# One block of an RWKV-7 layer: v's transposition moved, the last bonus moved, copies of the recurrence shared by ScalarE and VectorE

## The chip, the cores and the metric

The kernel runs on one core of a Trainium2 chip. The metric is the device time of one execution, in microseconds (us). The engines are named as in the profile: PE (TensorE, matrix products), DVE (VectorE), ACT (ScalarE), POOL (GpSimd) and SP (SyncE, which only issues DMAs here). Each engine works through its own queue in order, and a semaphore holds an instruction until what it needs is there.

## The reference, cut to what matters

One layer over 4096 tokens of width 1024, in fp32. An RMS-normalised, modulated input h is projected at once for a pooling branch and for the RWKV-7 branch (512 wide, 8 heads of 64). Around the change lies the second one:

```
seg = seg + (prev - seg) * mu_shift                  # each token mixed with the one before
r, w_lo, k, v, a_lo, z = split(seg)
decay = exp(-exp(-softplus(-(w0 + tanh(w_lo) @ w_up)) - 0.5))
a  = sigmoid(a0 + a_lo @ a_up);  kk = normalise(k * k_k);  k = k * (1 + (a - 1) * k_a)
# per head, token by token, S is 64 x 64:
sa = S @ (-kk);  S = S * decay + sa (kk * a)^T + v k^T;  y = S @ r
y  = groupnorm(y) * ln_w + ln_b
bonus = sum(r * k * r_k) * v
y_rwkv = (y + bonus) * silu(z)
out = concat(y_pool, y_rwkv) @ w_out;  x = rmsnorm(x + gate * out) * final_g
```

## The kernel before

The program has three stages. Until about 345 us it normalises x, transposes h to DRAM as two fp16 halves (high and low) and does the pooling branch (`proj`, L411 to L418). From there to about 1750 us it does the RWKV branch in 16 blocks of 256 tokens. Then comes the output projection (`project`, L923 to L965). The change lies in the middle stage.

A block has 4 chunks of 64 tokens and its 8 heads form 4 pairs. The recurrence is done chunk by chunk: within a chunk, the 64 steps are a triangular system, whose inverse is applied with matmuls. For each block b these functions run:

- `front(b, f)`, L542 to L649: a generator that projects the 17 segments of the block (pj, tile number m). Segment 0 holds the inputs of decay and a (lo), then pair p has k, r, v and z, m = 1+4p to 4+4p. A segment (`seg`) is 24 fp16 matmuls of 128x257 into a PSUM tile, evicted by an ACT activation (L561) and a DVE multiply-add with the shifted tokens (L562). After a pair's r segment come pl and pa (L588, L589), the tanh of both on ACT (tw, ta), the scan over time on DVE (L596) and the exponentials Ppad and Pi (L598, L600); after its v segment the DVE work that fills AR and BK, the operands of the scores (L608 to L619). Two closures remain from each pair: `cent`, which transposes v with two matmuls into vps (L629) and copies it with ACT into UV (L635), in the last pair with the squared norms of k (L632) as well, and `late`, which multiplies rk with a matrix of ones (pb, L642) and that by v on DVE (bon, L643). Both go on a list `todo`, which the next pair works off, `cent` ahead of its v segment and `late` behind it; those of the last pair are worked off in `scores`.
- `scores(b, f, fill)`, L651 to L693: for each chunk eight matmuls of BK with AR (scp), masked by DVE (L671), and in chunk 2 the norms (d2).
- `inverse`, L695 to L765: Ab is transposed out of the scores by DVE (L708), 30 dependent steps of two small DVE instructions follow (L726, L731), then the results are transposed, copied by ACT (MQ, L757) and completed by matmuls (qp, m21p); btp transposes BK on PE.
- `chain`, L795 to L865: for each chunk, the state S times AR (px, L814), two copies to SBUF (xa, L821), the matmuls with the inverse (psn, L826), two copies to SBUF (UV, L834), the update of the state (L842, and L848 on DVE), the output (L853) and two copies of it (y, L860). In each of these three pairs the two copies read the two halves of the partitions, one 64 x 256 each. Behind them runs the group norm of the output (gn, L866 to L878, with rstd on POOL at L875) and its transposition (ytp, L889) and last steps (mx, L891 to L893).

The front of block b+1 runs inside the other functions of block b: each `fill(n)` lets it issue n more steps, one k of a segment at a time. A scheduler then orders the instructions of each engine; some (`tc.high_priority`) are preferred, and the matmuls of the recurrence keep the order of the program. The pool of PSUM tiles `ps_pj` has three buffers, which pj, pl, pa, vps, pb and the output projection take in turn. So a new pj waits until the tile three before it has been read.

Of the kernel before, what the change touches and what calls it, by code (L numbers as in the profile page):

```python
# [25 lines left out]
HS = 64  # L26
# [26 lines left out]
def kernel(  # L53
# [29 lines left out]
    V, A, G, PE, SP = nc.vector, nc.scalar, nc.gpsimd, nc.tensor, nc.sync  # L83
# [56 lines left out]
    with ExitStack() as ph:  # L140
# [182 lines left out]
        for tok in plan.split():  # L323
            op, q = tok[0], int(tok[1:] or 0)
# [160 lines left out]
    with ExitStack() as ph:  # L485
# [56 lines left out]
        def front(b, f):  # L542
# [33 lines left out]
            todo = []  # L576
            sqs = []
            for p in range(NPAIR):
                kS = yield from seg(1 + 4 * p, "kS")
                sq = wk.tile([P, TB2], F32, tag=f"sq{p}", name=f"sq{b}_{p}")  # L580
                sqs.append(sq)
                A.activation(sq, kS, AF.Square, scale=vec[:, V_KK + p : V_KK + p + 1])
                yield
                rS = yield from seg(2 + 4 * p, "rS")

# [12 lines left out]
                A.activation(Pp[:, :, 1:], c3(L), AF.Exp, bias=0.0, scale=cexp)  # L598
                Pi = wk.tile([P, TB2], F32, tag="Pi", name=f"Pi{b}_{p}")
                A.activation(Pi, L, AF.Exp, bias=0.0, scale=-cexp)  # L600
                if todo:
                    todo.pop(0)()
                yield
                vS = yield from seg(3 + 4 * p, "vS")
                if p == 0:
# [39 lines left out]
                todo = [cent, late]  # L645
# [5 lines left out]
        def scores(b, f, fill):  # L651
            AR, BK = f["AR"], f["BK"]

            d2 = sm.tile([64, NI], F32, tag="d2", name=f"d2_{b}")
            d2T = sm.tile([P, 32], F32, tag="d2T", name=f"d2T{b}")
            sc = blk.tile([P, NI, P], F32, tag="sc", name=f"sc{b}")
            BT = blk.tile([P, NCH, 512], F32, tag="BT", name=f"BT{b}")
            for ch in range(NCH):

                pts = [pool.tile([P, 512], F32, tag=tg, name=f"scp{b}_{ch}_{tg}") for pool, tg in ((ps_sc, "sc"), (ps_x, "px"))]  # L660
                for j in range(4):
                    for hq in range(2):
                        o = 64 * hq
                        PE.matmul(  # L664
                            pts[hq][:, j * P : (j + 1) * P],
                            BK[o : o + 64, j, ch].rearrange("q a t -> q (a t)"),
                            AR[o : o + 64, j, ch].rearrange("q a t -> q (a t)"),
                            start=True, stop=True,
                        )
                for hq in range(2):  # L670
                    V.tensor_mul(  # L671
                        sc[:, ch * NH : (ch + 1) * NH, :].rearrange("q (j h) t -> q j h t", h=2)[:, :, hq],
                        pts[hq].rearrange("q (j t) -> q j t", j=4),
                        mask.unsqueeze(1).to_broadcast([P, 4, P]),
                    )
                fill(FS + 1)
                if ch == 2:
                    pt = ps_sc.tile([P, 512], F32, tag="sc", name=f"d2p{b}")
                    for c_ in range(NCH):
                        PE.transpose(pt[:64, c_ * P : (c_ + 1) * P], ssb[:, c_ * C : (c_ + 1) * C], ident)  # L680
                    V.tensor_scalar_max(
                        d2.rearrange("q (c p h) -> q c p h", c=NCH, h=2),
                        pt[:64].rearrange("q (c p e) -> q c p e", c=NCH, e=32)[:, :, :, 0:2], L2_EPS * L2_EPS,
                    )
                    V.reciprocal(d2, d2)
                    for g in range(2):
                        V.transpose(d2T[64 * g : 64 * g + 64], d2)
                if ch in (0, 3):
                    f["todo"].pop(0)()
                fill(FS)  # L690
                if ch % 2 == 0:
                    run(gns[0], 1)
            f["sc"], f["BT"], f["d2T"] = sc, BT, d2T  # L693
# [75 lines left out]
        def ordered(mm):  # L769

            pin[0] = True
            return tc.keep_in_program_order(mm)
# [22 lines left out]
        def chain(b, f, fill):  # L795
            AR, UV, sc, BT, pc = f["AR"], f["UV"], f["sc"], f["BT"], f["pc"]
            MT = UV[0:64].rearrange("q c (h t) -> q (c h) t", h=NH)
            pe, po = f["px"]
            uo = 4 * HS
            for ch in range(NCH):  # L800
                par = 256 * (ch % 2)

                psn = ps_s.tile([P, 512], F32, tag="psn", name=f"psn{b}_{ch}")
                if ch % 2 == 0:
                    y = blk.tile([P, 512], F32, tag="y", name=f"y{b}_{ch}", bufs=3)
                yv = y[64 * (ch % 2) : 64 * (ch % 2) + 64].rearrange("q (j f e) -> q j f e", f=2, e=HS)
                uv = UV[0:64, ch, :].rearrange("q (j f e) -> q j f e", f=2, e=HS)

                for p in range(NPAIR):
                    cs = slice(par + p * HS, par + (p + 1) * HS)  # L810
                    for ar in range(2):
                        for hf, px in ((0, pe), (1, po)):
                            o, ro = 64 * hf, 64 * (hf ^ ar)
                            ordered(PE.matmul(  # L814
                                px[ro : ro + 64, cs], AR[o : o + 64, p, ch, ar, :], S[o : o + 64, p, :],
                                start=(p == 0 and ar == 1), stop=(ar == 0), skip_group_check=True,
                            ))
                xa = blk.tile([64, 2, 256], F32, tag="W", name=f"xa{b}_{ch}")
                for hf, px in ((0, pe), (1, po)):
                    with tc.high_priority(offset=PRI):  # L820
                        A.copy(xa[:, hf, :], px[64 * hf : 64 * hf + 64, par : par + 256])  # L821
                fill(FA)
                nl = lead(b, f, ch + 1) if ch + 1 < NCH else iter(())
                for p in range(NPAIR):
                    for hf in range(2):
                        ordered(PE.matmul(  # L826
                            psn[64 * hf : 64 * hf + 64, uo + p * HS : uo + (p + 1) * HS],
                            MT[:, ch * NH + 2 * p + hf, :], xa[:, hf, p * HS : (p + 1) * HS],
                            start=True, stop=True, skip_group_check=True,
                        ))  # L830
                    run(nl, 1)
                for hf in range(2):
                    with tc.high_priority(offset=PRI):
                        A.copy(uv[:, :, hf], psn[64 * hf : 64 * hf + 64, uo:].rearrange("q (j e) -> q j e", e=HS))  # L834
                run(gns[0], 1)

                Sd = blk.tile([P, NPAIR, HS], F32, tag="Wt", name=f"Sd{b}_{ch}")
                V.tensor_mul(Sd, S, pc[:, :, ch : ch + 1].to_broadcast([P, NPAIR, HS]))
                fill(FB)
                for h in range(NH):  # L840
                    o, e = 64 * (h % 2), slice(h * HS, (h + 1) * HS)
                    ordered(PE.matmul(  # L842
                        psn[o : o + 64, (h // 2) * HS : (h // 2 + 1) * HS], BT[:, ch, e], UV[:, ch, e],
                        start=True, stop=True, skip_group_check=True,
                    ))
                with tc.high_priority(offset=PRI):
                    for p in range(NPAIR):
                        V.scalar_tensor_tensor(  # L848
                            S[:, p, :], psn[:, p * HS : (p + 1) * HS], pc[:, p, ch : ch + 1], Sd[:, p, :], op0=ALU.mult, op1=ALU.add,
                        )  # L850
                for h in range(NH):
                    hf, o = h % 2, 64 * (1 - h % 2)
                    ordered(PE.matmul(  # L853
                        (pe, po)[hf][o : o + 64, par + (h // 2) * HS : par + (h // 2 + 1) * HS],
                        sc[:, ch * NH + h, 64:128], UV[:, ch, h * HS : (h + 1) * HS],
                        start=False, stop=True, skip_group_check=True,
                    ))
                for hf, px in ((0, pe), (1, po)):
                    o = 64 * (1 - hf)
                    A.copy(yv[:, :, hf], px[o : o + 64, par : par + 256].rearrange("q (j e) -> q j e", e=HS))  # L860
                run(gns[0])
                if ch % 2 == 1:
                    gns[0] = gn(b, f, ch // 2, y)
                    run(gns[0], 1)
                fill(FY)  # L865
# [49 lines left out]
        def run(g, n=100000):  # L915
            for _ in range(n):
                if next(g, run) is run:
                    return
# [48 lines left out]
        gns = [iter(())]  # L967
        fs = {0: {}}
        run(front(0, fs[0]))
        for b in range(NB2):  # L970
            f = fs[b]
# [80 lines left out]
```

## Time and profile before

| what | us |
|---|---|
| median of 3 runs | 2130.35 |
| lowest and highest run | 2128.62, 2130.52 |
| the profiled execution | 2131.77 |
| its span | 2130.1 |

TensorE's mean granted clock over the span was 0.979 of full speed. The page gives each engine's busy time over the whole span. It says nothing of which engine sets the pace in a stage; that is read from the chain of waits and from what each engine waits for in one stretch. Times in the rows below are us from the span's start, one block of the middle stage being the stretch from 983.62 to 1068.53. The granted clock (PEclk) is a share of 2.4 GHz: 1.00 is that, 0.50 is 1.2 GHz.

### The profile page before, as it was taken

To read this page: it belongs to the slowest core of one execution; us is meant where nothing else is said; L and a number is where in the kernel's file an instruction comes from. 1 tells how busy PE (TensorE), PEld (TensorE's weight loads), DVE (VectorE), ACT (ScalarE), POOL (GpSimd) and SP (SyncE) were. 2 spreads that over 40 slices of the span, in tenths; PEclk is the share of its full clock that TensorE was granted. 3 is DMA by queue.
4 is the path that set the end of the run, shared out by engine and by line. 5 is a ranking of instruction groups with operands and counts; after the bars stand their busy time and mean duration, and the time that the engine had idled before them with its cause. 6 is when DMAs were issued, how large, how long until landed. Compare 5 with 4: busy or idle time off the path is not lost.

```text
span 2130.1 us, 48341 instructions
## 1 busy us (share of the span) xinstructions
PE 1984.4 (93%) x20186; PEld 1464.5 (69%) x20186; DVE 1454.7 (68%) x3549; ACT 966.0 (45%) x2119; POOL 148.3 (7%) x270
## 2 busy tenths in 40 slices
PE   3999999998999999999989999999899989999998
PEld 1544444577777777777777777777777767788886
DVE  7898877466867768678687686685776866533333
ACT  2544533244455554554555545545555453312111
POOL 3000000000000000000000000000001000100000
PEclk7999999999999999999999999999999999999999
DMA  7876767300100100101101001011010334443421
GB/s 277 279 237 208 256 209 268 97 21 2 32 27 6 31 15 18 32 2 31 27 6 31 23 10 32 2 31 27 7 31 27 134 111 140 150 142 133 152 106 69
DMA packets 140444, 183.19 MB, mean 86 GB/s; under 512 B 12097, under 2 KB 94017, under 8 KB 140226
## 3 DMA queue, kind: packets, MB, share of 16 engines
q1 hardware_dynamic: 140226, 180.11, 25.7%
q8 instruction: 158, 2.59, 0.5%
q14 instruction: 60, 0.49, 0.1%
HBM read 121.22 MB, written 58.85 MB: 85 GB/s over the span
## 4 chain that ended last, share of the span: by engine, by line
PE 54%; DVE 28%; ACT 10%; issue 4%; DMA 2%; POOL 0%; SPq 0%; DVEq 0%; ACTq 0%; POOLq 0%
PE po L952 6%; PE po L954 5%; PE po L953 5%; PE pj L557 5%; DVE W L731 4%; PE pj L559 4%; PE pj L558 4%; DVE Wt L726 4%; PE pp L415 4%; PE pp L416 4%; PE pp L417 4%; DVE Ab L708 3%; PE psn L826 2%; PE scp_sc L664 2%; PE px L814 2%
## 5 line engine op out<-in xcount | busy, mean ns | idle before, releaser
L557 PE MATMUL pj<-hh,w2h 128*128 128x257 f16 x2176 | 609.4, 280 | 49.8 <-DVE bon L643 23.9
L559 PE MATMUL pj<-hh,w2l 128*128 128x257 f16 x2176 | 603.9, 278 | 0.0
L558 PE MATMUL pj<-hl,w2h 128*128 128x257 f16 x2176 | 601.9, 277 | 0.0
L558 PEld LDWEIGHTS <-w2h 128*128 128x128 f16 x2176 | 217.5, 100 | 89.0 <-issue 59.1
L557 PEld LDWEIGHTS <-w2h 128*128 128x128 f16 x2176 | 214.8, 99 | 52.2 <-issue 6.5
L559 PEld LDWEIGHTS <-w2l 128*128 128x128 f16 x2176 | 213.4, 98 | 34.0
L952 PE MATMUL po<-wo,mh 128*128 128x512 f32 x512 | 204.3, 399 | 3.7 <-ACT mh L936 3.7
L953 PE MATMUL po<-wo,mh 128*128 128x512 f32 x512 | 201.9, 394 | 0.0
L416 PE MATMUL pp<-lo,w1h 128*128 128x512 f16 x512 | 195.1, 381 | 1.4 <-DVE lo L228 1.4
L415 PE MATMUL pp<-hi,w1h 128*128 128x512 f16 x512 | 194.9, 382 | 0.8 <-ACT hi L227 0.8
L417 PE MATMUL pp<-hi,w1l 128*128 128x512 f16 x512 | 195.0, 381 | 0.0
L956 DVE TENSOR_TENSOR x<-po,x 128x512 f32<-128x512 f32 x64 | 44.2, 690 | 151.5 <-PE po L954 151.4
L958 ACT ACTIVATE sq<-x 128x512 f32<-128x512 f32 x64 | 40.4, 631 | 209.2 <-DVE x L956 190.9
L726 DVE TENSOR_TENSOR Wt<-W,Ab 128x30 f32<-128x30 f32 (+7 forms) x480 | 117.6, 245 | 10.2
L731 DVE TENSOR_TENSOR W<-W,Wt 128x30 f32<-128x30 f32 (+7 forms) x480 | 117.5, 245 | 9.1
L952 PEld LDWEIGHTS po<-wo,mh 128*128 128x128 f32 x512 | 96.6, 189 | 26.0 <-ACT mh L936 3.9
L953 PEld LDWEIGHTS po<-wo,mh 128*128 128x128 f32 x512 | 96.6, 189 | 22.3
L954 PE MATMUL po<-wo,ml 128*128 128x512 f32 x256 | 101.5, 398 | 0.0
L562 DVE SCALAR_TENSOR_TENSOR kS<-pj,c,kS 128x256 f32<-128x256 f32 x64 | 30.6, 478 | 101.5 <-ACT kS L561 101.5
L417 PEld LDWEIGHTS <-w1l 128*128 128x128 f16 x512 | 50.3, 98 | 62.0 <-issue 2.8
L416 PEld LDWEIGHTS <-w1h 128*128 128x128 f16 x512 | 50.3, 98 | 60.1 <-issue 1.6
L415 PEld LDWEIGHTS <-w1h 128*128 128x128 f16 x512 | 50.4, 98 | 59.1 <-issue 1.2
(244 smaller groups left out, 3836.0 us busy)
## 6 DMA issues: line engine op xcount, KB each, us to landing
x<-in_x_dram SPq DMA_DIRECT2D x64, 256.0 KB, 2.9
out_dram<-x SPq DMA_DIRECT2D x64, 256.0 KB, 2.1
xk<-in_xT_dram SPq DMA_DIRECT2D x56, 256.0 KB, 3.8
xt<-in_x_dram SPq DMA_DIRECT2D x28, 512.0 KB, 5.6
wada<-in_w_ada_dram SPq DMA_DIRECT2D x24, 512.0 KB, 6.8
w2raw<-in_w_in_dram SPq DMA_DIRECT2D x17, 512.0 KB, 5.3
hh<-hT_hi SPq DMA_DIRECT2D x32, 257.0 KB, 3.6
hl<-hT_lo SPq DMA_DIRECT2D x32, 257.0 KB, 3.0
```

What stands on the lines that cost most here:

```text
L415: PE.matmul(pp, w1_hi[m][:, k, :], hi, start=(k == 0), stop=False)
L416: PE.matmul(pp, w1_hi[m][:, k, :], lo, start=False, stop=False)
L417: PE.matmul(pp, w1_lo[m][:, k, :], hi, start=False, stop=(k == KT - 1))
L557: unpin(PE.matmul(pp, w2_hi[m][:, k, :], hh[k], start=(k == 0), stop=False))
L558: PE.matmul(pp, w2_hi[m][:, k, :], hl[k], start=False, stop=False)
L559: PE.matmul(pp, w2_lo[m][:, k, :], hh[k], start=False, stop=(k == KT - 1))
L708: V.transpose(Ab[o : o + 32], sc[o : o + 32, :, o : o + 32].rearrange("s i t -> s t i"))
L726: V.tensor_mul(tmp[:, :n, :k], W[:, r0:, k : k + 1].to_broadcast([P, n, k]), Ab[:, k : k + 1, :k].to_broadcast([P, n, k]),)
L731: V.tensor_add(W[:, r0:, :k], W[:, r0:, :k], tmp[:, :n, :k])
L952: unpin(PE.matmul(po, mh[:, k, ts_], wo[0][k][n], start=(k == 0), stop=False))
L953: PE.matmul(po, mh[:, k, ts_], wo[1][k][n], start=False, stop=False)
L954: PE.matmul(po, (ml[:, k] if b % 2 == 0 else ml[k])[:, ts_], wo[0][k][n], start=False, stop=(k == KT - 1))
```

## The change

Three edits. `cent` of the pair before is worked off behind the next pair's k segment and no longer ahead of its v segment. `late` of the last pair is worked off in chunk 1 of the scores and no longer in chunk 3. And of each pair of copies in the recurrence (xa, UV, y) the second goes to DVE.

```diff
--- before.py
+++ after.py
@@ -580,6 +580,8 @@
                 sq = wk.tile([P, TB2], F32, tag=f"sq{p}", name=f"sq{b}_{p}")
                 sqs.append(sq)
                 A.activation(sq, kS, AF.Square, scale=vec[:, V_KK + p : V_KK + p + 1])
+                if todo:
+                    todo.pop(0)()
                 yield
                 rS = yield from seg(2 + 4 * p, "rS")
 
@@ -598,8 +600,6 @@
                 A.activation(Pp[:, :, 1:], c3(L), AF.Exp, bias=0.0, scale=cexp)
                 Pi = wk.tile([P, TB2], F32, tag="Pi", name=f"Pi{b}_{p}")
                 A.activation(Pi, L, AF.Exp, bias=0.0, scale=-cexp)
-                if todo:
-                    todo.pop(0)()
                 yield
                 vS = yield from seg(3 + 4 * p, "vS")
                 if p == 0:
@@ -685,7 +685,7 @@
                     V.reciprocal(d2, d2)
                     for g in range(2):
                         V.transpose(d2T[64 * g : 64 * g + 64], d2)
-                if ch in (0, 3):
+                if ch < 2:
                     f["todo"].pop(0)()
                 fill(FS)
                 if ch % 2 == 0:
@@ -816,9 +816,9 @@
                                 start=(p == 0 and ar == 1), stop=(ar == 0), skip_group_check=True,
                             ))
                 xa = blk.tile([64, 2, 256], F32, tag="W", name=f"xa{b}_{ch}")
-                for hf, px in ((0, pe), (1, po)):
+                for hf, px, cp in ((0, pe, A.copy), (1, po, V.tensor_copy)):
                     with tc.high_priority(offset=PRI):
-                        A.copy(xa[:, hf, :], px[64 * hf : 64 * hf + 64, par : par + 256])
+                        cp(xa[:, hf, :], px[64 * hf : 64 * hf + 64, par : par + 256])
                 fill(FA)
                 nl = lead(b, f, ch + 1) if ch + 1 < NCH else iter(())
                 for p in range(NPAIR):
@@ -829,9 +829,9 @@
                             start=True, stop=True, skip_group_check=True,
                         ))
                     run(nl, 1)
-                for hf in range(2):
+                for hf, cp in ((0, A.copy), (1, V.tensor_copy)):
                     with tc.high_priority(offset=PRI):
-                        A.copy(uv[:, :, hf], psn[64 * hf : 64 * hf + 64, uo:].rearrange("q (j e) -> q j e", e=HS))
+                        cp(uv[:, :, hf], psn[64 * hf : 64 * hf + 64, uo:].rearrange("q (j e) -> q j e", e=HS))
                 run(gns[0], 1)
 
                 Sd = blk.tile([P, NPAIR, HS], F32, tag="Wt", name=f"Sd{b}_{ch}")
@@ -855,9 +855,9 @@
                         sc[:, ch * NH + h, 64:128], UV[:, ch, h * HS : (h + 1) * HS],
                         start=False, stop=True, skip_group_check=True,
                     ))
-                for hf, px in ((0, pe), (1, po)):
+                for hf, px, cp in ((0, pe, A.copy), (1, po, V.tensor_copy)):
                     o = 64 * (1 - hf)
-                    A.copy(yv[:, :, hf], px[o : o + 64, par : par + 256].rearrange("q (j e) -> q j e", e=HS))
+                    cp(yv[:, :, hf], px[o : o + 64, par : par + 256].rearrange("q (j e) -> q j e", e=HS))
                 run(gns[0])
                 if ch % 2 == 1:
                     gns[0] = gn(b, f, ch // 2, y)
```

Two lines are added behind L582 and two taken out behind L600, so that in between a line of the changed kernel has a number two higher than before.

The order of instructions on DVE, in the recurrence of block 5, chunk 2 (Sd5_2, psn5_2), beside which the front of block 6 has its last pair (L611 to L619). Before:

```order
L872 TENSOR_REDUCE var5_0_11345<-ysq5_0_11343 128x8 [waits Activation_49]
L611 SCALAR_TENSOR_TENSOR BK6_10613<-tb6_3_11455,pv_3663,Pi6_3_11314 128x4x64 [waits DVE_49]
L873 TENSOR_SCALAR var5_0_11345<-var5_0_11345 128x8 [waits DVE_49]
L612 TENSOR_TENSOR ta6_3_11308<-ta6_3_11308,kS6_13_11207 128x256 [waits Activation_49]
L877 TENSOR_TENSOR y5_0_11155<-y5_0_11155,rstd5_0_11348 128x512 [waits Pool_49]
L613 TENSOR_TENSOR AR6_10375<-rS6_14_11299,Ppad1_3673 128x4x64
L614 TENSOR_TENSOR BK6_10613<-ta6_3_11308,Pi6_3_11314 128x4x64 [waits DVE_49]
L643 TENSOR_TENSOR bon6_10376<-pb6_2_11464,vS6_11_11009 128x256 [waits PE_49]
L619 SCALAR_TENSOR_TENSOR rk6_3_11467<-rS6_14_11299,pv_3663,ta6_3_11308 128x256
L848 SCALAR_TENSOR_TENSOR S_3678<-psn5_2_11357,pc5_9168,Sd5_2_11406 128x64 [waits PE_49,Activation_49]
```

After, with the copies of xa (L821) and UV (L834), each with what it waits for:

```order
L612 TENSOR_TENSOR ta6_3_11313<-ta6_3_11313,kS6_13_11207 128x256 [waits Activation_49]
L872 TENSOR_REDUCE var5_0_11345<-ysq5_0_11343 128x8 [waits Activation_49]
L821 COPY xa5_2_11375<-px5_1_11058 64x256 [waits PE_49]
L873 TENSOR_SCALAR var5_0_11345<-var5_0_11345 128x8 [waits DVE_49]
L613 TENSOR_TENSOR AR6_10375<-rS6_14_11304,Ppad1_3673 128x4x64
L877 TENSOR_TENSOR y5_0_11155<-y5_0_11155,rstd5_0_11348 128x512 [waits Pool_49]
L614 TENSOR_TENSOR BK6_10613<-ta6_3_11313,Pi6_3_11319 128x4x64
L643 TENSOR_TENSOR bon6_10376<-pb6_2_11464,vS6_11_11009 128x256
L834 COPY UV5_9169<-psn5_2_11357 64x4x64 [waits Activation_49]
L619 SCALAR_TENSOR_TENSOR rk6_3_11467<-rS6_14_11304,pv_3663,ta6_3_11313 128x256
L848 SCALAR_TENSOR_TENSOR S_3678<-psn5_2_11357,pc5_9168,Sd5_2_11406 128x64 [waits PE_49]
```

The UV copy stands behind L877, L614 and bon6 (L643), and waits for ACT.

On PE, at the start of the inverse of block 5: the last matmul of segment 2 of block 6, the matmuls of its first pair's decay (pl6_0, pa6_0) and the transpositions btp5. Before:

```order
L559 MATMUL pj6_2_10508<-hh6_1_10371,w2l2_959 128x257
L588 MATMUL pl6_0_10547<-lo6_0_10428,up_89 128x256
L718 MATMUL btp5_0_10561<-ident_80,BK5_9403 128x128 x4
L718 MATMUL btp5_1_10574<-ident_80,BK5_9403 128x128
L589 MATMUL pa6_0_10548<-lo6_0_10428,up_89 128x256
L718 MATMUL btp5_1_10574<-ident_80,BK5_9403 128x128 x3
L557 LDWEIGHTS w2h3_962
L557 MATMUL pj6_3_10567<-hh6_0_10367,w2h3_962 128x257
```

After:

```order
L559 MATMUL pj6_2_10511<-hh6_1_10371,w2l2_959 128x257
L590 MATMUL pl6_0_10547<-lo6_0_10428,up_89 128x256
L591 MATMUL pa6_0_10548<-lo6_0_10428,up_89 128x256
L718 MATMUL btp5_0_10561<-ident_80,BK5_9403 128x128 x4
L557 LDWEIGHTS w2h3_962
L557 MATMUL pj6_3_10567<-hh6_0_10367,w2h3_962 128x257
```

pl6_0 and pa6_0 now stand together, and the matmuls of btp5_1 follow later.

On PE, around the last pair's bonus of block 5 (pb5_3), which the scores of block 5 have worked off. Before, in segment 2 of block 6, behind the last matmuls of the scores:

```order
L558 MATMUL pj6_2_10508<-hl6_0_10369,w2h2_958 128x257
L559 LDWEIGHTS w2l2_959
L559 MATMUL pj6_2_10508<-hh6_0_10367,w2l2_959 128x257
L642 MATMUL pb5_3_10515<-rk5_3_10257,bones_3640 128x256
L557 LDWEIGHTS w2h2_958
L557 MATMUL pj6_2_10508<-hh6_0_10367,w2h2_958 128x257
```

After, between segments 0 and 1 of block 6, ahead of the matmuls of the scores' last chunks:

```order
L558 MATMUL pj6_0_10380<-hl6_1_10373,w2h0_950 128x257
L559 LDWEIGHTS w2l0_951
L559 MATMUL pj6_0_10380<-hh6_1_10371,w2l0_951 128x257
L642 MATMUL pb5_3_10432<-rk5_3_10257,bones_3640 128x256
L557 LDWEIGHTS w2h1_954
L557 MATMUL pj6_1_10435<-hh6_0_10367,w2h1_954 128x257
```

pb5_3 has moved ahead by about one segment and a half.

## Rows read from the trace of the kernel before

**Rows 1.** The page's first part, busy us, share of the span, instructions, by engine.

```profile
PE 1984.4 (93%) x20186; PEld 1464.5 (69%) x20186; DVE 1454.7 (68%) x3549; ACT 966.0 (45%) x2119; POOL 148.3 (7%) x270
```

**Rows 2.** Chain of waits, whole program: start us, duration us, engine, tile, line.

```profile
560.09 1.85 DVE Ab L708
...
983.62 1.85 DVE Ab L708
...
1068.53 1.86 DVE Ab L708
...
1152.60 1.85 DVE Ab L708
...
1661.28 1.85 DVE Ab L708
```

**Rows 3.** Stretches: start:end, length, busy (count) by engine, PEclk, DMA share, GB/s.

```profile
983.50:1025.60 42.10, 37.74 (x369) 30.41 (x367) 38.80 (x112) 21.00 (x46) 2.49 (x8) 0.96 0.03 7
1003.70:1007.00 3.30, 3.30 (x18) 2.35 (x16) 3.16 (x11) 1.32 (x3) 0.19 (x1) 0.50 0.00 0
1025.60:1051.20 25.60, 23.99 (x501) 18.09 (x499) 11.68 (x33) 17.86 (x47) 1.93 (x2) 1.00 0.03 7
1051.20:1068.50 17.30, 17.30 (x197) 14.17 (x196) 11.07 (x26) 6.17 (x16) 1.64 (x1) 1.00 0.28 73
```

**Rows 4.** DVE's waits in A: line, released by: us, times, longest us.

```profile
DVE vS L562 <- ACT vS L561: 0.8, 1, 0.8
DVE AR L610 <- ACT Ppad L598: 0.5, 1, 0.5
DVE szt L624 <- ACT tz L623: 0.5, 1, 0.5
```

**Rows 5.** PE's waits in one block, 985 to 1069, same columns.

```profile
PE pj L557 <- DVE bon L643: 1.7, 1, 1.7
PE vps L629 <- ACT tw L591: 1.7, 3, 0.6
PE pj L557 <- DVE rS L562: 1.2, 1, 1.2
PE psn L826 <- ACT xa L821: 0.4, 1, 0.4
PE pj L557 <- ACT UV L635: 0.4, 1, 0.4
```

**Rows 6.** Chain of waits at the end of A.

```profile
1024.71 0.41 DVE zS L562
...
1025.58 0.36 ACT MQ L757
```

**Rows 7.** Groups by shape: busy us, mean ns, idle before and its releaser.

```profile
L834 ACT COPY UV<-psn 64x256 f32<-64x256 f32 x128 | 47.1, 368 | 56.0 <-PE psn L826 55.2
...
L643 DVE TENSOR_TENSOR bon<-pb,vS 128x256 f32<-128x256 f32 x64 | 26.7, 418 | 2.2 <-PE pb L642 1.7
```

**Rows 8.** One line's instructions, L681: min, median, max ns, first and last start.

```profile
L681 DVE TENSOR_SCALAR d<-d2p x16: 173/183/183, 467.3 to 1739.5; 64x32 f32<-64x32 f32 x16
```

**Rows 9.** Timeline of B and C: start us, us, engine, line, instruction, idle before.

```profile
1038.57 0.71 PE L629 MATMUL vps<-cmat,vS 128*128 128x128 f32 x4 [0.56 <-ACT tw L591]
...
1042.14 0.69 PE L814 MATMUL px<-S,AR 64*64 64x64 f32 x30
...
1043.52 1.74 POOL L875 TENSOR_TENSOR rstd<-var,nhalf 128x8 f32<-128x8 f32 x1 [2.77 <-DVE var L873]
...
1045.30 0.69 DVE L877 TENSOR_TENSOR y<-y,rstd 128x512 f32<-128x512 f32 x1 [1.53 <-POOL rstd L875]
...
1045.38 0.69 PE L842 MATMUL psn<-UV,BT 128*64 128x64 f32 x16
...
1066.10 0.60 PE L642 MATMUL pb<-rk,bones 128*128 128x256 f32 x2
...
1066.53 0.27 PE L557 MATMUL pj<-hh,w2h 128*128 128x257 f16 x1
```

## The prediction

> **What bounds the kernel now.** I read the page's busy shares first: PE 93%, DVE 68%, ACT 45% [rows 1]. That invites "PE is the bound, so every wait of PE is time". The stages tell another story, so I went on to the chain of waits over the whole program, which passes each block's first transposition of the inverse (Ab): from 983.62 to 1068.53 is 84.91 us, from 1068.53 to 1152.60 is 84.07, and the 13 blocks from 560.09 to 1661.28 take 84.71 on average [rows 2]. I call such a distance a period; 15 blocks have a following block's front inside them, and the change acts on these.
>
> One period falls into three stretches [rows 3]. In A, 42.1 us (inverse), DVE is busy 38.80 and PE 37.74; in B, 25.6 us (recurrence), PE 23.99, ACT 17.86, DVE 11.68; in C, 17.3 us (scores), PE is busy throughout. Of A the waits of DVE show only 1.8 us (0.8, 0.5, 0.5) [rows 4]: A is as long as DVE's queue, and it ends with zS and the copy of MQ [rows 6]. PE's waits are 5.4 us a block (1.7 for bon, 1.7 for tw in three pieces, 1.2 for rS, twice 0.4) [rows 5], but all but a few tenths of them lie in A, where PE has 42.1 − 37.74 = 4.4 us to spare and DVE sets the end. What PE does not wait for bon or rS, it waits for MQ.
>
> The periods of 84.91 and 84.07 differ in the granted clock. From 1003.7 to 1007.0, behind PE's waits in A, it was 0.50, that is 1.2 GHz; in B and C it was 1.00 [rows 3]. So one fall costs 84.91 − 84.07 = 0.84 us, and the mean period says that it comes (84.71 − 84.07) / 0.84 = 0.76 times a block.
>
> **The change part by part.** *Stretch A.* The bonus of the last pair (one DVE multiplication from PSUM, 0.42 us [rows 7]) leaves the head of A for C: −0.4, since DVE is what A waits for. The 1.7 us for which PE waited on it go too; they were hidden behind DVE. In PE's queue pl and pa, the inputs of tw and ta, then stand together (second pair of pieces of order), and v's transposition stands one segment earlier, where it waits for other evictions. What is late next there is rS and tw, through the same three buffers of PSUM, and then MQ. I count −0.4 and nothing for PE. If that cover were gone, the 5.4 us would be open; that is the first rival.
>
> *Stretch B.* Of six copies in each chunk three go from ACT to DVE: 3 × 4 × 16 = 192. On ACT each takes 0.37 us [rows 7], and a pair runs one behind the other. On DVE the trace shows no copy of 64x256 from PSUM. The nearest rows are 0.18 us for 64x32 from PSUM [rows 8] and 0.42 for 128x256 from PSUM with a second operand [rows 7]; I take 0.42, the row of the same free size, and keep 0.18 for the range. So a pair that runs side by side takes 0.42 instead of some 0.75: at most −0.35 for each, if DVE is free at that moment. Whether it is, the order says, chunk by chunk:
>
> - In all chunks the DVE copy of UV waits for ACT's copy of the same UV (the first pair of pieces of order shows it, the wait on Activation at L834). That pair stays serial: 0, or +0.05 by 0.42 against 0.37.
> - Chunk 0: the pair for xa gains some 0.35, but UV loses and PE's leftover work fills the rest: the next L814 is 0.14 earlier.
> - Chunk 1: v's transposition no longer stands before the recurrence matmul L842; the wait for tw there was 0.56 [rows 9], and its work of 0.4 leaves as well, while the xa copy stands behind the scan. L814 of chunk 2 starts some 1.5 earlier than before.
> - Chunk 2: here DVE's queue bites. The UV copy now stands behind L877, which waits for POOL's rstd, 1.74 us long [rows 9], and behind L614 and bon. From px at about 1041.3 (1.5 earlier): xa copy 0.42, L873 about 0.2, POOL 1.74 and its semaphores 0.2, L877 0.69 [rows 9], L614 and bon 0.8, UV copy 0.42: L842 starts between 1045.8 and 1046.2, against 1045.38 [rows 9], although the chunk began 1.5 earlier. PE stands still some 2.2 us of it. L814 of chunk 3 is 0.4 later than before.
> - Chunk 3: xa stands behind L892, which waits for ACT (+0.2); the pairs of xa and y give 0.35 each. The end of B comes 0.4 + 0.2 − 0.7 = −0.1; I take −0.15.
>
> ACT is relieved by 192 × 0.37 = 71 us, and DVE takes 192 × 0.42 = 81 us, 5 us a block, into B where it has 25.6 − 11.68 = 13.9 to spare. Neither sets B.
>
> On the UV pair there is a rule that would ask for more. The two halves read partitions 0 to 63 and 64 to 127 of one bank. The Trainium skill, "PSUM — Partial Sum Buffer", section "PSUM bank collisions raise a hardware error", says that two engines may use one bank at the same moment if they are in different quadrants of 32 partitions; by that rule the pair could run side by side, some 0.3 × 15 = 5 us less in all where nothing else waits. The program holds a wait all the same, so the sum goes by the wait; no row of before shows two engines reading one bank.
>
> *Stretch C.* The bonus's matmul (two pieces) stood behind the matmuls that Ab needs, and now stands ahead of them, in chunk 1 (third pair of pieces): from 1066.10 to the next matmul at 1066.53 it costs PE 0.43 [rows 9]. C has no idle PE to hide it: +0.43. Its DVE part falls where DVE is busy 11.07 of 17.3 and costs nothing.
>
> *Clock.* PE's waits in A are cut, which favours the clock; in B one wait of 2.2 us is made in chunk 2, where none was. I take one fall a block in place of 0.76: a period of 84.07 − 0.4 − 0.15 + 0.43 + 0.84 = 84.79 against 84.71, and 15 × 0.08 = 1.2 us.
>
> *Ends.* In the front of the first block v's transposition moves too and PE's queue has other segments around it; the last block has the copies without a front: 0 for both, by less than 1 us each.
>
> The profiled run took 2131.77 us (span 2130.1), 1.42 above the median of 2130.35. 2131.77 + 1.2 − 1.42 = 2131.6: forecast 2132.
>
> Bounds of the unknown: copies at 0.18 would save 0.24 on some six copies of a block that others wait for (four of xa, two of y), 1.4 × 15 = 21 us, so about 2111. Falls of the clock from none to two a block: −0.84 to +0.84 around the forecast, ±13 us.
>
> **The rivals.**
>
> *1. PE is the bound after all.* Then the 5.4 us of waits [rows 5] all come back: 15 × 5.4 = 81, so 2050. For it speaks the 93%; against it 38.80 of 42.1 us of DVE in A and the 1.8 us that DVE waits there.
>
> *2. The clock stays up.* With bon gone from the head of A, and PE's waits there spread over more and shorter pieces, no stretch at 0.50 follows. The period is 83.95, 0.76 below 84.71: 15 × 0.76 = 11, so 2119. For it: one fall per block is all there is before, and it came behind waits that the change shortens. Cheaper copies on DVE than 0.42 would end in the same place. Against it: rS and the tw waits stay, and chunk 2.
>
> *3. Slower: DVE's queue in the recurrence.* The UV copy of chunk 2 stands behind POOL's rstd, PE idles about 2.2 us in B, where it had idled 1.6 us in all four chunks together, and the clock falls there as well as in A: two falls in place of 0.76 and 1.0, +0.9 over the forecast with the wait's own rest: 15 × 0.9 = 13.5, so 2145. It decides from where the granted clock in B drops to 0.50 in more than one block of three (then +0.3 × 15 = 4.5 us, past what I call no change). Against it: POOL's 1.74 us begins only 0.2 us behind xa's copy, so it may end sooner than I reckon.
>
> *4. The change doesn't do what it says.* The UV pair stays serial and the waits of PE move to other names (rS for bon, MQ for rS): that is contained in the forecast, at about the old time.
>
> **How the numbers follow.** A measurement of this kernel can tell about 0.2% from no change: 2126.1 to 2134.6 is "the same". Forecast (A −0.4, B −0.15, C +0.43, one fall): chance 0.38, its own range 2124 to 2140 from half a fall either way and copies between the two prices in part; of it 0.28 within the bound, 0.04 faster, 0.06 slower. Rival 1: 0.04, faster. Rival 2: 0.30, faster. Rival 3: 0.26, slower. A remainder of 0.02, slower, for what I don't see. So faster 0.38, same 0.28, slower 0.34. The range leaves out rival 1 and the tails: 2112, near the cheap copies' end, to 2148, just above rival 3.
>
> **What would show each step.** Right: no wait of pj for bon, in the head of A; A shorter by some 0.4 us with DVE still waiting less than 2 us in it; C longer by some 0.4; the DVE copies at about 0.42; L842 of chunk 2 behind a UV copy that follows L877; one stretch at 0.50 a block. Wrong: A shorter by more than 1 us (PE was the bound there), DVE copies at 0.2 to 0.3, a DVE UV copy beside ACT's, B shorter by over 1 us (rival 2, or cheap copies) or stretches at 0.50 in B (rival 3).

## The result and the profile after

The changed kernel takes 2205.03 us (median of 4 runs, 2203.11 to 2209.26) against 2129.51 for the kernel before beside it: a ratio of 1.0357, interval 1.0342 to 1.0371. It is 3.6% slower; 2132 was forecast, with 2112 to 2148 as the range.

The period from Ab to Ab in the chain of waits (start, duration, engine, tile, line), beside [rows 2]:

```profile
561.69 1.85 DVE Ab L708
...
1007.67 1.86 DVE Ab L708
...
1098.13 1.84 DVE Ab L708
...
1189.98 1.85 DVE Ab L708
...
1277.37 1.86 DVE Ab L708
...
1729.34 1.85 DVE Ab L708
```

It is now 90.46, 91.85 and 87.39 us in turn, and 89.82 on average over the same 13 blocks, 5.1 more than 84.71. These 13 periods make 66 of the 71 us by which the two profiled spans differ (2201.4 against 2130.1); the medians differ by 75.5. The block from 1007.67 in stretches, beside [rows 3] (start:end, length, busy by engine, PEclk, DMA share, GB/s): inverse up to the MQ copy, recurrence, scores, and two pieces of the recurrence.

```profile
1007.60:1048.50 40.90, 36.30 (x372) 29.97 (x371) 38.33 (x110) 19.97 (x45) 2.52 (x8) 1.00 0.03 8
1048.50:1080.80 32.30, 29.14 (x500) 21.37 (x500) 16.40 (x44) 14.32 (x37) 1.93 (x2) 0.84 0.04 11
1080.80:1098.00 17.20, 17.20 (x192) 14.06 (x192) 11.73 (x27) 5.76 (x14) 1.64 (x1) 1.00 0.24 61
1051.80:1055.00 3.20, 3.20 (x43) 2.28 (x42) 0.38 (x2) 1.29 (x4) 0.00 (x0) 0.50 0.03 5
1072.40:1078.90 6.50, 6.50 (x62) 4.39 (x60) 3.41 (x9) 2.61 (x7) 0.00 (x0) 0.50 0.00 0
```

The inverse is 1.2 us shorter than in [rows 3], and its granted clock is 1.00. The recurrence takes 32.3 us. Here it is cut at L842 of chunk 3; with the same cut the kernel before took 26.0 for it and 16.95 from there to the next Ab, for which this one takes 17.37. The recurrence holds two stretches at 0.50, which fill the last two windows, and PE idles 3.2 us in it. Of what PE waits for in this block, beside [rows 5] (line, released by: us, times, longest):

```profile
PE m21p L763 <- ACT MQ L757: 1.4, 1, 1.4
...
PE ytp L889 <- DVE y L877: 1.2, 1, 1.2
...
PE psn L842 <- DVE UV L834: 0.8, 1, 0.8
```

The bonus's wait is gone, as foreseen. These three waits are new. Of the others of the block one, 0.3 us for xa, lies in the recurrence (0.4 before); the rest are for tw, zS, vS, rS and kS, 3.7 us in all and in the inverse. The last two of the rows lie in chunk 2, in the timeline beside [rows 9]:

```profile
1067.03 0.43 DVE L821 COPY xa<-px 64x256 f32<-64x256 f32 x1
...
1067.61 1.75 POOL L875 TENSOR_TENSOR rstd<-var,nhalf 128x8 f32<-128x8 f32 x1 [6.49 <-DVE var L873]
...
1068.22 0.37 ACT L834 COPY UV<-psn 64x256 f32<-64x256 f32 x1 [1.42 <-PE psn L826]
...
1069.39 0.69 DVE L877 TENSOR_TENSOR y<-y,rstd 128x512 f32<-128x512 f32 x1 [1.53 <-POOL rstd L875]
...
1070.14 0.44 PE L889 MATMUL ytp<-ident,y 128*128 128x128 f32 x2 [1.17 <-DVE y L877]
...
1070.88 0.43 DVE L834 COPY UV<-psn 64x256 f32<-64x256 f32 x1
...
1071.36 0.69 PE L842 MATMUL psn<-UV,BT 128*64 128x64 f32 x16 [0.79 <-DVE UV L834]
```

ACT has copied its half of UV by 1068.59. DVE's half waits behind L877 (for rstd), L614 and bon until 1070.88, so that L842 starts 63.69 us behind Ab, where it started 1045.38 − 983.62 = 61.76 behind it. The copy of UV on DVE, beside [rows 7]:

```profile
L834 DVE COPY UV<-psn 64x256 f32<-64x256 f32 x64 | 27.3, 426 | 71.0 <-ACT UV L834 69.8
```

Its price, 0.43 us, is the one taken (0.42); the copy of xa takes as long.

### The profile page after: what moved, and what is told of

Same layout as the page of the kernel before. It is cut to its first block, busy times and chain, and to the rows that moved or that the text cites. A ratio compares the mean times of both kernels' runs of the same rounds, so it can differ in the third digit from the quotient of the medians.

```text
span 2201.4 us, 48300 instructions
## 1 busy us (share of the span) xinstructions
PE 2028.6 (92%) x20186; PEld 1500.0 (68%) x20186; DVE 1535.3 (70%) x3741; ACT 887.0 (40%) x1927; POOL 148.7 (7%) x270
## 4 chain that ended last, share of the span: by engine, by line
PE 53%; DVE 34%; ACT 5%; issue 4%; DMA 2%; POOL 2%; SPq 0%; DVEq 0%; ACTq 0%; POOLq 0%
PE po L952 5%; PE po L954 5%; PE po L953 5%; PE pj L557 4%; DVE W L731 4%; DVE Wt L726 4%; PE pp L417 4%; PE pp L416 4%; PE pp L415 4%; PE pj L559 4%; PE pj L558 4%; DVE Ab L708 3%; PE scp_sc L664 2%; DVE L L598 2%; PE px L814 2%
## 5 line engine op out<-in xcount | busy, mean ns | idle before, releaser
L664 PE MATMUL scp_sc<-AR,BK 64*128 64x128 f32 x512 | 84.6, 296 | 0.0
```

What stands on the lines that cost most here:

```text
L664: PE.matmul(pts[hq][:, j * P : (j + 1) * P], BK[o : o + 64, j, ch].rearrange("q a t -> q (a t)"), AR[o : o + 64, j, ch].rearrange("q a t - ...
```

## The experiments

Medians in us; each ratio is against runs of the kernel before on the same chip (2129.5 to 2131.8, so a difference of two runs on different chips is good to some 2 us). Theory 1: DVE's copy of UV behind rstd makes PE idle in chunk 2, and the clock falls behind it. Theory 2: the moved parts let PE run dry at the end of the inverse.

**e1, copies of UV on ACT again.** In the changed kernel:

```diff
-                for hf, cp in ((0, A.copy), (1, V.tensor_copy)):
+                for hf in range(2):
                     with tc.high_priority(offset=PRI):
-                        cp(uv[:, :, hf], ...
+                        A.copy(uv[:, :, hf], ...
```

> The changed kernel with both copies of UV (L834) on ACT again; xa and y stay shared, v's transposition and the last bonus stay moved. Theory 1 (the DVE copy of UV in chunk 2 stands behind L877, which waits for POOL's rstd; PE idles before L842 and the clock then falls a second time in two blocks of three): L842 of chunk 2 comes some 2 us earlier after the block's Ab, stretches at 0.50 in chunk 2 to 3 go, 2.3 us of wait and on average 2.4 us of clock leave each of 15 blocks: about 2135, 2125 to 2145. Theory 2 (the moved transposition and bonus let PE run dry at the end of the inverse, so that the clock falls in the recurrence, and the copies matter little): 2185 to 2205.

2146.19, ratio 1.0076 (1.0059 to 1.0093): 59 us come back, and no block has a second stretch at 0.50. L842 of chunk 2 starts 61.3 us behind Ab in place of 63.6 to 63.7. Theory 1 holds, but the time is 11 us above its 2135 and 1 above its range: xa and y cost something too.

**e2, the three copies alone** (the kernel before with the last three hunks of the change).

> The kernel before with the copies shared (xa, UV, y) and nothing else changed. Theory 1: most of the loss is here, 2190 to 2210. Theory 2: 2120 to 2140, as the moved parts are missing.

2144.97, 1.0071 (1.0056 to 1.0086). Neither theory had this: without the moved parts the copies lose 15 us, with them 95 (see e3). In this kernel's chunk 2 DVE's UV stands directly behind L877, without L614 and bon between; PE waits 1.4 us there (ytp 1.1, L842 0.3) in place of 2.0, and its recurrence has no stretch at 0.50 in any block behind the first: a block without one takes 85.1 to 85.2 us against 84.07. So the parts are not to be added up.

**e3, both moved parts alone** (the first three hunks).

> The kernel before with v's transposition and the last bonus moved, all copies of the recurrence on ACT. Theory 1: no wait before L842 of chunk 2, period of a block between 83.8 and 85, 2120 to 2137. Theory 2: the loss is here, 2170 to 2205.

2109.84, 0.9904 (0.9889 to 0.9919): 20 us faster, better than either theory said, and theory 2 falls. Chunk 1 of its recurrence:

```profile
1106.32 1.04 PE L814 MATMUL px<-S,AR 64*64 64x64 f32 x32
...
1110.42 0.69 PE L842 MATMUL psn<-UV,BT 128*64 128x64 f32 x16
```

From L814 to L842 it takes 4.10 us. Before, it took 5.41:

```profile
1033.80 1.08 PE L814 MATMUL px<-S,AR 64*64 64x64 f32 x32
...
1039.21 0.69 PE L842 MATMUL psn<-UV,BT 128*64 128x64 f32 x16
```

This gain of 1.3 is most of the 1.5 that the prediction gave to chunk 1. The changed kernel has lost it again:

```profile
1057.70 0.33 PE L814 MATMUL px<-S,AR 64*64 64x64 f32 x2
...
1057.95 0.70 PE L590 MATMUL pl<-lo,up 64*128 64x256 f32 x2
...
1059.73 0.69 DVE L598 TENSOR_TENSOR_SCAN L<-rst,tw 128x256 f32<-128x256 f32 x1 [1.64 <-ACT tw L596]
...
1060.46 0.43 DVE L821 COPY xa<-px 64x256 f32<-64x256 f32 x1
...
1062.95 0.69 PE L842 MATMUL psn<-UV,BT 128*64 128x64 f32 x16
```

There pl has moved between L814's halves, and the DVE copy of xa stands behind the scan: 5.25 us.

**e4, L877 without the wait for rstd.** In the changed kernel, the group norm's last factor being left out:

```diff
-                rstd.unsqueeze(2).to_broadcast([P, NH, HS]),
+                var.unsqueeze(2).to_broadcast([P, NH, HS]),
```

> The changed kernel, but L877 multiplies y with var in place of rstd, so that the group norm's last factor is left out of the output and L877 waits for nothing but DVE; POOL still computes rstd. The order of all engines is that of the changed kernel. Theory 1: DVE's copy of UV in chunk 2 starts about 1.5 us earlier, PE's waits before L842 (1.2 for ytp, 0.8 for UV) shrink to under 0.6, the second stretch at 0.50 goes: 15 times 1.5 to 3.9 us less than 2205, 2145 to 2180. Theory 2: no change beyond 0.3%, 2198 to 2211.

2147.80, 1.0083 (1.0068 to 1.0098): 57 us less. L842 of chunk 2 (Ab at 989.15):

```profile
1049.25 0.68 DVE L877 TENSOR_TENSOR y<-y,var 128x512 f32<-128x512 f32 x1
...
1050.73 0.43 DVE L834 COPY UV<-psn 64x256 f32<-64x256 f32 x1
...
1051.21 0.69 PE L842 MATMUL psn<-UV,BT 128*64 128x64 f32 x16 [0.56 <-DVE UV L834]
```

62.06 behind Ab, 1.6 less, with the queues in the order of the changed kernel; the periods are 85.9 and 87.2, with one stretch at 0.50 each, in the second twice as long. So the wait for rstd itself is 1.5 us of a period (87.39 − 85.86, both with one short stretch), some 23 us in 15 blocks; the other 34 go with the second stretches at 0.50, which came behind it. In the changed kernel's block of 87.39 L842 starts 63.6 us behind Ab too, and no second stretch follows; what decides whether one does, no run here showed.

**e5, v's transposition moved alone; e6, the last bonus moved alone** (the first two hunks of the diff, and the third).

> The kernel before with v's transposition moved alone. Theory 1 (the 1.5 us won in chunk 1 of the recurrence come from v's transposition leaving the place before L842): L842 of chunk 1 some 1.5 us earlier than before, 15 times 1.2 to 1.6 less than 2130: 2104 to 2113. Rival (the gain of the run with both moved parts came from the bonus's wait): 2124 to 2134.

> The kernel before with the last bonus moved alone. Theory 1: inverse 0.3 shorter, scores 0.43 longer, one stretch at 0.50 a block: 2126 to 2136. Rival (the gain of the run with both moved parts came from the bonus's wait): 2106 to 2116.

e5: 2114.28, 0.9919 (0.9903 to 0.9936), the lowest run 2108.81: 1 us above the range of theory 1 and 10 below the rival's. e6: 2138.51, 1.0038 (1.0025 to 1.0051). The gain is the transposition's. The bonus alone loses 8 us, 2.5 past its range: in ten of 14 blocks the stretch at 0.50 in the inverse is now the longer kind (85.4 to 85.6 us a period, with the short one 85.0).

**e7, of the copies only xa; e8, only y** (with both moved parts).

> Both moved parts, and of the copies only xa shared with DVE. In the order of this kernel the scan of the last pair stands behind chunk 1's copy, as with all copies on ACT. Theory 1 (a shared copy gains 0.3 us where DVE is free and loses what stands ahead of it where it is not): two or three of four chunks gain 0.3, chunk 3 is held by L892: 2095 to 2113. Rival (any copy on DVE costs, by the way between engines): 2118 to 2135.

> Both moved parts, and of the copies only y shared with DVE. Here the copy of y stands behind the four state updates, and pl of the last pair and the scan have moved ahead as in the changed kernel. Theory 1: L814 of chunk 1 is 0.5 to 1.2 us longer than with all copies on ACT, since its second half waits for DVE: 2118 to 2135. Rival (the copies of xa are what costs the 36 us between both moved parts alone and with xa and y shared): 2104 to 2114.

e7: 2138.77, 1.0035 (1.0022 to 1.0048); e8: 2123.58, 0.9962 (0.9950 to 0.9975). Against e3 xa costs 29 us and y 14. For y theory 1 holds. For xa the time lies above both ranges, and theory 1 as I had worked it out was wrong in both halves. In chunks 0 and 1 the copy stands free and gains nothing (L842 of chunk 1 starts 54.10 us behind Ab, in e3 54.07): PE has the front's matmuls between L814 and L826, and these hid ACT's second copy. Nor does the copy cost anything there, as the rival would have it. In chunk 3 it costs much more than 0.2:

```profile
1053.73 0.36 ACT L821 COPY xa<-px 64x256 f32<-64x256 f32 x1
...
1053.93 0.48 DVE L619 SCALAR_TENSOR_TENSOR rk<-rS,pv,ta 128x256 f32<-128x256 f32 x1
...
1054.32 0.68 DVE L892 TENSOR_TENSOR mx<-mx,bon 128x512 f32<-128x512 f32 x1
...
1054.93 0.48 DVE L562 SCALAR_TENSOR_TENSOR vS<-pj,c,vS 128x256 f32<-128x256 f32 x1
1055.44 0.43 DVE L821 COPY xa<-px 64x256 f32<-64x256 f32 x1
...
1055.92 0.68 PE L826 MATMUL psn<-xa,UV 64*64 64x64 f32 x14 [0.94 <-DVE xa L821]
```

ACT's half is done at 1054.09. DVE first works off rk, L892 and vS, and PE waits 0.94 us for its half in the middle of L826.

**e9, of the copies only UV.** With both moved parts.

> Both moved parts, and of the copies only UV shared with DVE. In chunk 2 the DVE copy stands behind L877 (rstd) as in the changed kernel, and the copy of xa does not stand ahead of L873. Theory 1 (the wait for rstd, and the clock behind it, are UV's own): L842 of chunk 2 some 1 to 2 us later than with all copies on ACT, a second stretch at 0.50 in part of the blocks: 2135 to 2190. Rival (UV alone would be ready in time; it takes xa in front of L873, which delays rstd, to make it late): 2108 to 2125.

2159.43, 1.0128 (1.0113 to 1.0143): 50 us against e3, without xa or y. Theory 1 holds, and here the wait is the larger part: L842 of chunk 2 starts 62.3 us behind Ab (in e3 59.8), a period with one short stretch is 86.1 (in e3 83.4 to 83.5), and only four of 15 blocks have a second stretch.

**e10, xa shared in chunks 0 to 2.** In e7's kernel:

```diff
-... ((0, pe, A.copy), (1, po, V.tensor_copy)):
+... ((0, pe, A.copy), (1, po, V.tensor_copy if ch < NCH - 1 else A.copy)):
```

> Both moved parts, xa shared with DVE in chunks 0 to 2 and on ACT alone in chunk 3. Theory 1 (the loss of the kernel with xa shared everywhere is made in chunk 3, behind L892, 1.2 to 1.4 us a block, and the rest, 0.36, in chunk 2): 2112 to 2122. Rival (a copy on DVE costs in each chunk): 2128 to 2138.

2127.94, 0.9985 (0.9976 to 0.9995). 11 us come back of e7's 29, fewer than expected: the time is 6 us above theory 1's range and at the lower end of the rival's. The rival's reason does not show: L842 of chunks 0 to 2 comes within 0.2 us of e3's. The period with a short stretch at 0.50 is 83.8 to 84.0, 1.2 to 1.4 below e7's 85.2, which is chunk 3's loss. But in ten of 14 blocks the stretch behind the inverse is now twice as long, and those periods are 85.0 to 85.3. Why it lasts longer there stays open.

**e11, fill of the inverse.** With both moved parts and all copies on ACT:

```diff
-    FS, FE, FT, FQ, FA, FB, FY = 2, 2, 12, 4, 3, 2, 2
+    FS, FE, FT, FQ, FA, FB, FY = 2, 2, 10, 6, 3, 2, 2
```

> Both moved parts, all copies on ACT, and two of the front's steps moved from ahead of qp to behind it (FT, FQ from 12, 4 to 10, 6), so that ACT's MQ copies stand ahead of the eviction of z and its tanh. Theory 1 (the stretch at 0.50 that now stands at the end of the inverse comes behind PE's wait for MQ): the wait of m21p falls from 1.4 us to under 0.8, the stretches at 0.50 go or become rare: 2085 to 2104. Rival (the clock falls on other waits, or the time comes back behind m21p): 2106 to 2116.

2069.78, 0.9704 (0.9688 to 0.9720): the fastest kernel here, 3.0% faster than before and better than expected. The end of the inverse, first in the timeline of the changed kernel:

```profile
1045.38 0.75 PE L755 MATMUL qp<-MQ,sc 32*32 32x32 f32 x64
...
1047.59 0.47 DVE L562 SCALAR_TENSOR_TENSOR zS<-pj,c,zS 128x256 f32<-128x256 f32 x1
1048.10 0.42 ACT L623 ACTIVATE tz<-zS 128x256 f32<-128x256 f32 x1 [1.95 <-DVE zS L562]
1048.54 1.53 ACT L757 COPY MQ<-qp 32x256 f32<-32x256 f32 x4
```

and then in that of e11:

```profile
998.65 0.75 PE L755 MATMUL qp<-MQ,sc 32*32 32x32 f32 x64
...
999.74 1.53 ACT L757 COPY MQ<-qp 32x256 f32<-32x256 f32 x4
...
1002.33 0.42 ACT L623 ACTIVATE tz<-zS 128x256 f32<-128x256 f32 x1 [0.55 <-DVE zS L562]
```

Between qp and ACT's copy of MQ lay 3.16 us, in which ACT's queue held tz (the tanh for z, L623) and tz waited for DVE's zS. With two steps of the front moved behind qp it is 1.09, and no block with a front but the first has a stretch at 0.50. The chain of waits:

```profile
961.62 1.84 DVE Ab L708
...
1042.20 1.85 DVE Ab L708
```

80.6 us a period, against 82.7 in e3 without such a stretch and 83.5 with a short one.

**e12, ytp in the order of the program.** In the changed kernel, `ordered(PE.transpose(...))` at L889.

> The changed kernel with ytp's transpositions (L889) kept in the order of the program, so that they stand behind L853 and no longer between L826 and L842 in chunk 2; DVE's order is as in the changed kernel. Theory 1 (DVE's copy of UV sets L842, ytp only waits beside it): L842 of chunk 2 within 0.2 us of the changed kernel, 2190 to 2212. Rival (the transposition that waits for y is what holds PE's queue): L842 0.5 us or more earlier, fewer stretches at 0.50, 2140 to 2185.

2198.87, 1.0323 (1.0308 to 1.0338). Its timeline in chunk 2:

```profile
1077.77 1.12 PE L842 MATMUL psn<-UV,BT 128*64 128x64 f32 x16 [2.18 <-DVE UV L834]
```

ytp no longer stands ahead of L842, and PE waits for DVE's UV in one piece of 2.18 us. L842 starts 1077.77 − 1014.04 = 63.73 us behind Ab, as in the changed kernel (63.69). The copy sets it, not ytp.

**e13, the changed kernel with e11's fill; e14, the kernel before with it; e15, v's transposition alone with it.**

> The changed kernel with the fill of the inverse as in the fastest kernel so far (FT, FQ of 10, 6). Theory 1 (the loss in chunk 2 and 3 is the recurrence's own and independent of the stretch at 0.50 at the end of the inverse): 2.7 us of inverse and 0.7 of clock go, chunk 2's wait stays: 2140 to 2165, still 70 to 95 above the kernel with both moved parts and this fill. Rival (the second stretch at 0.50 needs the first wait): both go, 2105 to 2130.

> The kernel before with the fill of 10, 6 alone. If ACT's MQ copies behind z's tanh set the end of the inverse there too: 2 to 3 us a block less, 2085 to 2103. If the end of DVE's own work sets it: 2118 to 2132.

> v's transposition moved alone, with the fill of 10, 6. Against both moved parts with this fill: scores 0.43 us shorter (the last bonus stands behind what Ab needs), inverse 0.3 to 0.7 longer, stretches at 0.50 behind the bonus's wait at the head of the inverse hidden: 2064 to 2080.

e13: 2141.42, 1.0051 (1.0036 to 1.0066), in theory 1's range: the copies lose 72 us against e11, where they lost 95 against e3. Behind the wait in chunk 2 the clock still falls, in nine of 14 blocks, without a fall ahead of it:

```profile
1050.00:1053.20 3.20, 3.20 (x27) 2.30 (x23) 1.82 (x7) 2.13 (x6) 0.00 (x0) 0.50 0.00 0
```

Its chain of waits, with this block and the one ahead of it, in which the clock stays at 1.00:

```profile
904.64 1.84 DVE Ab L708
...
988.84 1.85 DVE Ab L708
...
1074.56 1.85 DVE Ab L708
```

So a short stretch at 0.50 in this place costs 85.72 − 84.20 = 1.5 us. And 84.20 is 3.6 above e11's 80.6 without any fall: some 54 of the 72 us that the copies lose here are waits and order, without the clock.

e14: 2121.46, 0.9956 (0.9940 to 0.9973), within what I gave to DVE's bound, but the rows show another:

```profile
1016.78 1.22 DVE L745 STREAM_TRANSPOSE MQ<-UV 32x1024 f32<-32x1024 f32 x1
...
1021.48 0.75 PE L755 MATMUL qp<-MQ,sc 32*32 32x32 f32 x64
...
1022.27 1.53 ACT L757 COPY MQ<-qp 32x256 f32<-32x256 f32 x4 [1.59 <-PE qp L755]
```

MQ's transposition is done at 1018.00, and qp comes 3.5 us later, behind the other matmuls in PE's queue: ACT, with tz out of its way, waits 1.59 us for PE. e15: 2086.31, 0.9794 (0.9779 to 0.9808), 6 above its range and 17 above e11: with this fill the bonus at the head of the inverse costs more (MQ's copy comes 1.9 us later in the block, and 1.05 where no stretch at 0.50 lies ahead of it) than its place in the scores.

## Why the prediction was wrong

*Stretch A*, −0.4: MQ's copy starts 1048.54 − 1007.67 = 40.87 behind Ab, before 1025.58 − 983.62 = 41.96 in a block with a stretch at 0.50 [rows 2, 6]. Of these −1.1 the clock's share is 0.84, and some −0.25 is left: right in size, and too simple as a reading. The inverse had two limits close together, PE's queue up to qp and DVE's up to zS, behind which ACT holds tz and the MQ copy. Taking PE's early waits out alone leaves the second (changed kernel, e3: 3.16 us between qp and the copy, PE dry at m21p, the clock falling at the start of the recurrence). Taking tz out of the way alone leaves the first (e14, 8 us); behind the moved transposition it is worth 28 us (e15 against e5), behind both moved parts 40 (e11 against e3). So rival 1 was half right: PE's waits were worth something, once the limit beside them was gone. Of PE's 5.4 us of waits, besides, 1.0 lay in the recurrence (0.6 for tw, 0.4 for xa), not a few tenths.

*Stretch C*, +0.43: right (17.37 against 16.95 behind the last L842, and 17.38 in e3).

*Stretch B*, −0.15, is the step that failed first; the number and the price of the clock's falls are the second. In the block of 87.39, with one short stretch at 0.50, B takes 29.2 us from MQ's copy to the last L842, where the kernel before took 26.0 at full clock. Some 0.8 of these 3.2 is the stretch itself (e3: 83.5 against 82.7 us a period), which lay in A before; 2.4 are waits and order, where −0.15 was forecast. B failed in four terms.
- *Chunk 1*, −1.5: e3, e7 and e9 show it (3.9 to 4.1 us from L814 to L842), but all with y on ACT. With y on DVE pl moves between L814's halves (e8 too, 4.7 us), the copy of xa stands behind the scan, and 0.2 is left.
- *Chunk 2*, L842 0.8 later by my sum up to 1046.2: it is 63.69 − 61.76 = 1.9 later. The mechanism was named; the main part of L814 came 0.5 us earlier (1065.71 − 1007.67 = 58.04, before 58.52 [rows 9]) and not 1.5, and the copy of xa, which rstd follows, waited for L872's 0.68. L872 stood in the order and I did not charge it.
- *Chunk 3*, −0.5 for its pairs: the copy behind rk, L892 and vS cost 1.4 a block (e7 against e10).
- *Pairs side by side*, −0.35 each: nothing in chunks 0 and 1 (e7), because the front's matmuls hid the second copy. I had argued this way for PE's waits in A and not for ACT's copies in B.

*Clock.* One fall a block for 0.84: ten of the 15 blocks have two, which adds 89.82 − 87.39 = 2.4 us on average. The price of 0.84 was read for a short stretch in the inverse, where DVE sets the pace and part of PE's slowness is hidden. A stretch as short behind chunk 2 costs 1.5 (e13), and most of the second stretches are twice as long: 90.46 − 87.39 = 3.1 us. So place and length make up the difference, each by a factor of about two. Rival 3 was the right mechanism, down to the place, at 0.9 a block; by e4 it is 1.5 of wait and 34/15 = 2.3 of clock. Of the 6.3 us a block between e3 and the changed kernel ((2205.03 − 2109.84) / 15) the other 2.5 are xa's and y's: e1 against e3 is 36 us, 2.4 a block.

*The bank.* DVE's copy of UV keeps waiting for ACT's, as the program has it: the two never read psn side by side in the rows above. The Trainium skill, "PSUM — Partial Sum Buffer", section "PSUM bank collisions raise a hardware error", would allow it for different quadrants; no run here tried it.

## What to carry to other kernels

A copy handed to a less busy engine is worth what ends last there: look first whether the copy it shortens is waited for at all, then charge it with every instruction ahead of it in the new queue and with what those wait for. Take the price of a fall of the clock from the stage in which it will come, and look how long it lasts: one read where another engine is the bound, or from a shorter fall, is too low. And parts of a change are to be tried apart: here one part alone gained 17 us, and three together lost 75.

## What the runs showed of the hardware that was not expected

The stretches at 0.50 came in two lengths. In the changed kernel one at the start of the recurrence and one in chunks 2 and 3 fill windows of 3.20 and 6.50 us (above); in e3 there are both, and periods of 82.7 without one (same columns as above):

```profile
931.40:937.90 6.50, 6.45 (x138) 5.16 (x139) 0.00 (x0) 3.26 (x9) 0.00 (x0) 0.50 0.01 3
1016.70:1019.90 3.20, 3.20 (x52) 2.15 (x42) 0.00 (x0) 2.19 (x6) 0.00 (x0) 0.50 0.00 0
```

The period with the longer is 84.6 us, with the shorter 83.5: 1.9 and 0.8 more. In chunks 2 and 3 the shorter cost 1.5 (e13) and the longer 3.1 (changed kernel). What decides between the lengths no run here showed.
